# Reloads moved from GpSimd to ScalarE, U's copy taken from PSUM, and first loads on two queues, in a two-block transformer kernel

## The chip, the cores and the metric

The kernel runs on one core of one Trainium2 chip. The metric is the device time of one execution in microseconds (us). Three runs of the kernel before gave 2861.27, 2851.15 and 2854.03 us, median 2854.03. The profiled execution, from which all times in the prediction come, took 2851.9 us.

The names used below: PE is TensorE (matmuls and transposes), ACT is ScalarE, DVE is VectorE, POOL is GpSimd, SP is SyncE, which here only issues transfers. Each engine works through its own instructions in a fixed order. A DMA is issued by an instruction of one of these engines and then runs by itself.

## The reference, cut to what matters

The input is one sequence of 256 tokens of width 2048, all in float32. Two transformer blocks follow each other. The first mixes RWKV-7 time mixing (16 heads) with dilated attention (16 heads):

```python
def first_block(x, ...):
    u = rms_norm(x, norm1_g)
    q, k, v, z = split(u @ w_in)                       # attention 3 x 1024, RWKV 3360 columns
    attn = dilated_attention(q, k, v, rel_bias_table)  # three windows, joined by their log-sum-exp
    rw = rwkv7_time_mix(z, ...)
    h = x + concat([attn, rw]) @ w_out
    return rms_norm(h + ffn(rms_norm(h)), final_g)

def rwkv7_step(state, inp):                            # 256 steps, one after the other
    r, w, k, v, a, bb = inp
    sa = einsum('bhij,bhj->bhi', state, a)
    state = state * w + sa[..., None] * bb + v[..., None] * k
    y = einsum('bhij,bhj->bhi', state, r)
```

`rwkv7_time_mix` ends with a group norm of y over each head (mean, variance, reciprocal root), a bonus term and a gate. The second block has three other attention branches, a gated merge and a feed-forward part with a short convolution. Its order of work is not touched here.

## The kernel before, in words

**The weight products.** Nearly all of the time goes into `lin` (L299): out[256, n] = x @ W in float32 precision, made of three products in a faster number format. Of each weight tile of 128x512 float32 (`raw`, loaded by SP, 512 KB for two tiles, three buffers), ACT casts the high part `wh` (L332, three buffers), DVE subtracts the low part `wl` (L333, two buffers), and PE multiplies x's high part by `wh` and by `wl`, and x's low part by `wh`: six matmuls of 512 columns for a weight tile, three for each half of the tokens (L219). The x tiles themselves are split once into high and low parts; for the first block this is `load_T` (L1104), which loads x transposed in eight pieces, splits each on ACT (L1114) and DVE (L1115), then loads x in its natural order and squares it on ACT (L254) for the row norm.

**RWKV in chunks.** The 16 heads are done in four groups of four heads. For each group, keys, receptances and values are brought in from a DRAM spool (`spool`, L982; w_in's products are written there by ACT, and `load`, L997, brings them back as kA, rA, vA for group 1, kB, rB, vB for groups 2 and 3), transposed on PE into `zt`, and turned into matrices over chunks of 32 tokens: D, BKT and others (`rwkv_pairs`). For each chunk a triangular system has to be solved: `solve_T` (L578) sends D through DRAM (scN) into a layout N, runs 62 small dependent operations on POOL (31 multiplications X, L594, and 31 additions T, L596), and sends the result through DRAM (scT) to the tile TTx, of which there is one. Then `chain` (L604) runs the eight chunks, each depending on the one before. One step of it is: a D matmul (`ch<-UV,D`), copies Xc by DVE and ACT (L625, L626), a TTx matmul (`ch<-Xc,TTx`), copies into UV by DVE and ACT (L628, L629), a BKT matmul (`ch<-UV,BKT`), a copy of U into Ux by POOL (L636), a matmul `ch<-Ux,D`, the new state S on DVE (L640, L641) and the output copy Y on ACT (L644), with which the next step's `ch<-S,ARx` begins. All the matmuls of a step write into one PSUM tile, `ch`. There are 32 steps in all, 8 for each of 4 groups.

**After a chain.** `rwkv_out` (L650) does the group norm of Y on DVE and ACT, transposes it on PE (`yt`), multiplies by the gate (`g` on PE) and gives `rw`. For groups 0 to 2 POOL writes rw to DRAM (`mixd`, L687) and later loads it back as `mx` (L1078), as it does with the attention outputs; ACT and DVE split it into `mixh` and `mixl` (L1084, L1085), the inputs of the output product `lin("w_out")`. Group 3's rw is split in place. Pairs of k-tiles of w_out stand for the pieces: 10 and 11 for the last attention quarter, 12 and 13 for group 2, 14 and 15 for group 3.

**What sets the order.** The program is written stage by stage. A scheduler with a model of time then puts all instructions of a core in an order for each engine, with `high_priority(SPLIT_AHEAD)` drawing the raw loads and weight splits of `lin` forward. So independent `lin` matmuls stand on PE between the steps of a chain. Once built, each engine keeps its order: an instruction that waits holds up all those behind it on its engine, DMA issues too. The reloads of kA and the others, the mx loads, the solver and the Ux copies all stand in POOL's one order.

**Startup.** `pv` (a table of gains and other small parameters) is loaded by POOL; ACT issues the eight loads of x transposed (`x<-in_xT` in the profile) and the eight of x natural; POOL clears many tiles (memsets, L383 and others).

Of the kernel before, what the change touches and what calls it, by code (L numbers as in the profile page):

```python
# [19 lines left out]
P = 128  # L20
S = 256
# [66 lines left out]
NPV = _c  # L88
# [96 lines left out]
class Builder:  # L185
    def __init__(self, ctx, tc, A, dbg=None):
# [9 lines left out]
        self.woff = {}  # L196
        self.pvt = self.load_const("pv", [P, NPV], eng=self.nc.gpsimd)
        self.ident = self.load_const("c_ident", [P, P], eng=self.nc.gpsimd)
# [151 lines left out]
class Block1(Builder):  # L350
# [253 lines left out]
    def chain(self, st):  # L604
# [10 lines left out]
        for c in range(8):  # L615
# [15 lines left out]
            if c < 7:  # L631
# [3 lines left out]
                l = lc[:, :, c, :].to_broadcast([P, 2, 64])  # L635
            nc.gpsimd.tensor_copy(Ux[0:64], by(st.UV)[0:64, :, c, :])  # L636
            for p in range(2):
# [329 lines left out]
class Kernel(Block2):  # L967
# [14 lines left out]
    def spool(self, name):  # L982
# [14 lines left out]
        def load(half):  # L997
            t = self.slot([P, 2, S], name)
            nc.gpsimd.dma_start(t, d[:, :, half * S:(half + 1) * S])
            return t  # L1000
# [5 lines left out]
    def block1_mix(self):  # L1006
        nc, tc = self.nc, self.tc
        with tc.tile_pool(name="ring1", bufs=1) as self.ring, tc.tile_pool(name="p1", bufs=1) as self.p1:
            self.NW, self.NWL = 3, 2
            xT = self.new_xT("x")  # L1010
            ss = self.new_ss("x", 8)
            self.load_T(xT, "x", "norm1_g", ss, nc.scalar)
            rs = self.row_rstd(ss, "x")
# [3 lines left out]
            self.lin("w_in", 0, xT, self.nat_evac(lo, rs))  # L1017
            self.rwkv_consts()
            self.lora_lo(lo)
# [83 lines left out]

    def load_T(self, xT, name, gain, ss, queue):  # L1104

        nc = self.nc
        hi, lo = xT
        for c in range(8):
            t = self.slot([P, 2, S], name) if name == "x" else self.stage(name)
            queue.dma_start(t, self.A[name + "T"][:, 2 * c:2 * c + 2, :])  # L1110
            for j in range(2):
                kt = 2 * c + j
                g = self.pv(gain, kt)
                nc.scalar.activation(hi[:, kt, :], t[:, j, :], AF.Identity, scale=g)  # L1114
                nc.vector.scalar_tensor_tensor(lo[:, kt, :], t[:, j, :], g, hi[:, kt, :].bitcast(F32),  # L1115
                                               op0=ALU.mult, op1=ALU.subtract)
        for c in range(8):
            t = self.stage(name)
            queue.dma_start(t, self.A[name][:, c * S:(c + 1) * S].rearrange("(t p) c -> p t c", p=P))
            for tb in range(2):  # L1120
                self.square(ss, t[:, tb, :], tb, c)
# [4 lines left out]
    def mem_kv(self):  # L1126
# [3 lines left out]
        ss = self.new_ss("mem", 8)  # L1130
        self.load_T(xT, "mem", "g_mem_2", ss, nc.gpsimd)
        rs = self.row_rstd(ss, "mem")
# [193 lines left out]
```

## Time and profile before

| | |
|---|---|
| runs | 2861.27, 2851.15, 2854.03 us, median 2854.03 |
| profiled execution | 2851.9 us, of which the span of the profile is 2850.1 |
| PE busy | 2773.8 us, 97% of the span |
| DVE, ACT, POOL busy | 1741.2 (61%), 1550.3 (54%), 179.7 (6%) |
| DMA | 534.37 MB, mean 187 GB/s |

In the profile's lists a row names the line, the engine and the operation, `out<-in` by the program's tile names; `x12` counts instructions. In a timeline a row begins with the start and the duration in us, and `[4.53 <-DMA kA<-sp_kA]` says that the engine stood idle for 4.53 us before it, until this transfer had landed. PE shows as busy from a matmul's start to its modelled end, and matmuls overlap. PEld is the loading of the stationary operand, PEclk the granted TensorE clock as a share of full speed.

### The profile page before, as it was taken

Reading aid. Unit: us, or ns where it says so; the run is one execution under the profiler, and the core shown is the slowest. Engines: PE = TensorE matmul, PEld = TensorE weight load, DVE = VectorE, ACT = ScalarE, POOL = GpSimd, SP = SyncE. Lnnn points to the kernel's source line nnn. Section 1 sums busy time; section 2 is a strip of 40 time slices with the busy share of each in tenths; the row PEclk is TensorE's granted clock in tenths of the full one; section 3 lists DMA queues with packets and bytes.
Section 4 is the critical chain, followed back from the end, with each engine's and each line's share of the span. In section 5 each row is a group of like instructions: output and inputs, shape, how many; then the busy total and the mean of one; then the engine's idle time right before and its main releaser. Section 6 shows DMA issues by size and latency. Waiting matters only on the chain.

```text
span 2850.1 us, 40071 instructions
## 1 busy us (share of the span) xinstructions
PE 2773.8 (97%) x13496; PEld 2320.1 (81%) x13496; DVE 1741.2 (61%) x3088; ACT 1550.3 (54%) x2847; POOL 179.7 (6%) x395
## 2 busy tenths in 40 slices
PE   7989989999999999999999999999999999999999
PEld 6877877777888888888888888888888888888887
DVE  5665756557555555555666666666666666667554
ACT  5544546546544445454555664455556666666444
POOL 2034043300000000000000000000000000000000
PEclk9999999999999999999999999999999999999999
DMA  6755556565666666666655556666555555555665
GB/s 212 208 166 169 179 153 204 168 217 175 191 191 190 188 189 190 192 190 191 217 174 181 163 170 193 199 203 196 190 184 188 185 185 185 185 184 185 200 201 168
DMA packets 168663, 534.37 MB, mean 187 GB/s; under 512 B 31041, under 2 KB 36167, under 8 KB 168456
## 3 DMA queue, kind: packets, MB, share of 16 engines
q1 hardware_dynamic: 149404, 487.90, 54.7%
q0 software_dynamic: 7360, 25.28, 2.9%
q10 hardware_dynamic: 11692, 18.63, 2.0%
q8 instruction: 106, 1.74, 0.3%
q14 instruction: 101, 0.83, 0.1%
HBM read 518.07 MB, written 16.82 MB: 188 GB/s over the span
## 4 chain that ended last, share of the span: by engine, by line
PE 89%; DMA 4%; POOL 2%; issue 2%; DVE 2%; ACT 1%; SPq 0%; ACTq 0%; DVEq 0%; POOLq 0%
PE lin L219 83%; PE ch L648 1%; POOL T L596 1%; POOL X L594 1%; PE tr L224 1%; PE uT L224 1%; DMA scN<-D 1%; DMA N<-scN 1%; DVE wl L333 0%; DMA x<-in_xT_dram 0%; PE o L219 0%; PE D L219 0%; DMA raw<-in_w_out_dram 0%; DMA mem<-in_memT_dram 0%; PE lg L219 0%
## 5 line engine op out<-in xcount | busy, mean ns | idle before, releaser
L333 DVE TENSOR_TENSOR wl<-raw,wh 128x512 fp32r<-128x512 f32 (+2 forms) x1848 | 1268.1, 689 | 891.9 <-PE lin L219 780.9
L332 ACT CAST wh<-raw 128x512 fp32r<-128x512 f32 (+2 forms) x1848 | 1138.9, 618 | 1098.5 <-PE lin L219 1027.8
L219 PE MATMUL lin<-wl,x2h 128*128 128x512 f32 (+2 forms) x800 | 293.3, 369 | 3.1 <-DVE wl L333 3.1
L219 PE MATMUL lin<-wh,x2l 128*128 128x512 f32 (+2 forms) x800 | 289.4, 364 | 0.0
L219 PE MATMUL lin<-wl,u2h 128*128 128x512 f32 x704 | 281.0, 399 | 0.0
L219 PE MATMUL lin<-wl,hhi 128*128 128x512 f32 x704 | 275.0, 391 | 0.0
L219 PE MATMUL lin<-wh,u2l 128*128 128x512 f32 x704 | 274.3, 390 | 0.0
L219 PE MATMUL lin<-wh,hlo 128*128 128x512 f32 x704 | 273.9, 389 | 0.0
L219 PE MATMUL lin<-wl,uh 128*128 128x512 f32 x704 | 273.9, 391 | 0.0
L219 PE MATMUL lin<-wh,ul 128*128 128x512 f32 x704 | 272.7, 390 | 0.4 <-DVE ul L291 0.4
L219 PE MATMUL lin<-wh,x2h 128*128 128x512 f32 (+2 forms) x800 | 244.9, 365 | 1.6 <-ACT wh L332 1.2
L219 PE MATMUL lin<-wh,uh 128*128 128x512 f32 x704 | 227.7, 391 | 1.0 <-ACT uh L290 0.9
L219 PE MATMUL lin<-wh,u2h 128*128 128x512 f32 x704 | 225.6, 392 | 0.0
L219 PE MATMUL lin<-wh,hhi 128*128 128x512 f32 x704 | 219.9, 389 | 0.0
L219 PE MATMUL lin<-wl,xh 128*128 128x512 f32 (+2 forms) x512 | 191.5, 378 | 8.1 <-DVE wl L333 8.0
L219 PE MATMUL lin<-wh,xl 128*128 128x512 f32 (+2 forms) x512 | 180.2, 356 | 0.0
L219 PEld LDWEIGHTS lin<-wl,x2h 128*128 128x128 f32 x800 | 150.8, 189 | 29.1 <-DVE wl L333 6.1
L219 PE MATMUL lin<-wh,xh 128*128 128x512 f32 (+2 forms) x512 | 154.0, 359 | 18.3 <-ACT wh L332 18.3
L219 PEld LDWEIGHTS lin<-wh,x2h 128*128 128x128 f32 x800 | 148.0, 188 | 26.5 <-ACT wh L332 1.8
L219 PEld LDWEIGHTS lin<-wh,x2l 128*128 128x128 f32 x800 | 150.9, 189 | 22.8
L219 PEld LDWEIGHTS lin<-wh,uh 128*128 128x128 f32 x704 | 132.1, 188 | 29.6 <-ACT uh L290 1.7
L219 PEld LDWEIGHTS lin<-wh,u2h 128*128 128x128 f32 x704 | 132.2, 188 | 27.9
(428 smaller groups left out, 3786.8 us busy)
## 6 DMA issues: line engine op xcount, KB each, us to landing
raw<-in_w_in_dram SPq DMA_DIRECT2D x268, 512.0 KB, 3.8
raw<-in_w_gate_up_dram SPq DMA_DIRECT2D x176, 512.0 KB, 3.8
raw<-in_w_down_dram SPq DMA_DIRECT2D x176, 512.0 KB, 4.0
raw<-in_w_up_dram SPq DMA_DIRECT2D x176, 512.0 KB, 3.6
raw<-in_w_out_dram SPq DMA_DIRECT2D x64, 512.0 KB, 3.7
raw<-in_w_mem_kv_dram SPq DMA_DIRECT2D x16, 512.0 KB, 4.2
raw<-in_w_br_fox_dram SPq DMA_DIRECT2D x12, 512.0 KB, 4.2
raw<-in_w_br_sb_dram SPq DMA_DIRECT2D x12, 512.0 KB, 4.3
```

The source lines that it names most:

```text
L219: self.nc.tensor.matmul(out, lhsT=lhsT, rhs=rhs, start=start, stop=stop)
L224: self.nc.tensor.transpose(out, in_, self.ident[p0:p0 + n, p0:p0 + n])
L332: nc.scalar.copy(wh[:, :m * n], raw[:, cs])
L333: nc.vector.tensor_tensor(wl[:, :m * n], raw[:, cs], wh[:, :m * n].bitcast(F32), op=ALU.subtract)
L594: gp.tensor_tensor(x, T[:, 0:m, u:u + 1].to_broadcast([P, m, n]), N[:, u:u + 1, u + 1:32].to_broadcast([P, m, n]), op=ALU.mult)
L596: gp.tensor_tensor(w, w, x, op=ALU.add)
L648: self.nc.tensor.matmul(out, lhsT=lhsT, rhs=rhs, start=start, stop=True, skip_group_check=True)
```

## The change

Three parts are changed.

1. **First loads.** pv is loaded by ACT, as its first transfer. All eight loads of x transposed are issued ahead of the splits, alternately by ACT and by SP (between SP's first raw weights). The RWKV constants (with POOL's memsets) stand between the splits of x and the natural loads, and the natural loads are issued by POOL. `SPLIT_AHEAD = 100` draws the first weight splits forward.
2. **U's copy.** Ux is written by one ACT copy and one DVE copy of 64x64, each straight from the PSUM tile `ch`, where POOL copied 64x128 out of UV. In the built program the ACT copy waits for the BKT matmuls on PE, which write the same PSUM tile, the DVE copy waits for the ACT copy, and the matmul `ch<-Ux,D` for the DVE copy.
3. **Reloads.** kA, rA, vA, kB, rB, vB (kB, rB and vB twice) are issued by ACT.

```diff
-        self.pvt = self.load_const("pv", [P, NPV], eng=self.nc.gpsimd)
+        self.pvt = self.load_const("pv", [P, NPV], eng=self.nc.scalar)
...
-            nc.gpsimd.tensor_copy(Ux[0:64], by(st.UV)[0:64, :, c, :])
+            nc.scalar.copy(Ux[0:64, 0, :], ch[0:64, 128:192])
+            v.tensor_copy(Ux[0:64, 1, :], ch[64:128, 128:192])
...
         def load(half):
             t = self.slot([P, 2, S], name)
-            nc.gpsimd.dma_start(t, d[:, :, half * S:(half + 1) * S])
+            nc.scalar.dma_start(t, d[:, :, half * S:(half + 1) * S])
...
-            self.load_T(xT, "x", "norm1_g", ss, nc.scalar)
+            self.SPLIT_AHEAD = 100
+            self.load_T(xT, "x", "norm1_g", ss, (nc.scalar, nc.sync), self.rwkv_consts)
...
-            self.rwkv_consts()
             self.lora_lo(lo)
...
-    def load_T(self, xT, name, gain, ss, queue):
+    def load_T(self, xT, name, gain, ss, queues, between=None):
...
+        def load(c):
+            ts.append(self.slot([P, 2, S], name) if between else self.stage(name))
+            queues[c % len(queues)].dma_start(ts[c], self.A[name + "T"][:, 2 * c:2 * c + 2, :])
+
+        if between:
+            for c in range(8):
+                load(c)
         for c in range(8):
-            t = self.slot([P, 2, S], name) if name == "x" else self.stage(name)
-            queue.dma_start(t, self.A[name + "T"][:, 2 * c:2 * c + 2, :])
+            if not between:
+                load(c)
+            t = ts[c]
...
+        if between:
+            between()
         for c in range(8):
             t = self.stage(name)
-            queue.dma_start(t, self.A[name][:, c * S:(c + 1) * S].rearrange("(t p) c -> p t c", p=P))
+            nc.gpsimd.dma_start(t, self.A[name][:, c * S:(c + 1) * S].rearrange("(t p) c -> p t c", p=P))
```

The change also moves instructions in the scheduler's order. Three places matter to the prediction.

**PE at the end of group 2's chain.** Numbers behind a name tell one tile from the next: before, `ch_4250` is group 3's chain, `Y_3908` group 2's output, and group 2's chain has ended ahead of the first row. The rows before:

```order
L219 MATMUL lin_5731<-wh_5832,mixl_5650 128x512
L224 MATMUL ot_5156<-k_c_ident,on_5075 128x128 x2
L648 MATMUL ch_4250<-UV_4060,BKT_4059 128x64 x2
L648 MATMUL ch_4250<-Ux_402,D_4058 128x64 x2
L224 MATMUL yt_4230<-k_c_ident,Y_3908 128x128 x4
L219 MATMUL g_4231<-gT,gup 128x256 x4
L648 MATMUL ch_4250<-S_4261,ARx_397 128x64 x2
L648 MATMUL ch_4250<-UV_4060,D_4058 128x64 x2
```

The rows of the changed kernel, where `ch_3925` is group 2's chain and `ch_4274` group 3's:

```order
L649 MATMUL ch_3925<-Xc_4027,TTx 128x64
L219 MATMUL lin_5924<-wh_5928,mixh_5681 128x512
L649 MATMUL ch_3925<-UV_3409,BKT_3408 128x64 x2
L649 MATMUL ch_3925<-Ux_159,D_3407 128x64 x2
L649 MATMUL ch_3925<-S_4035,ARx_152 128x64 x2
L649 MATMUL ch_3925<-UV_3409,D_3407 128x64 x2
L649 MATMUL ch_3925<-Xc_4047,TTx 128x64
L649 MATMUL ch_3925<-UV_3409,BKT_3408 128x64 x2
L649 MATMUL ch_3925<-Ux_158,D_3407 128x64 x2
L649 MATMUL ch_3925<-S_4055,ARx_152 128x64 x2
L649 MATMUL ch_3925<-UV_3409,D_3407 128x64 x2
L649 MATMUL ch_3925<-Xc_4067,TTx 128x64
```

Behind these come `ch_3925<-Ux_159` (group 2's last), four entries of group 3's chain, group 2's `yt` and `g`, seven more entries of group 3's chain, and only then the next weight matmul, of k-tile 12. Between group 2's last `ch<-Ux` and its `yt` there stood 28 weight matmuls of 512 columns before; there stands none now. In an average step of the chains 2.5 weight matmuls stood between the BKT matmul and `ch<-Ux`; there stand 10.1 now.

**PE at the end of group 3's chain**, the last one. The rows before, in which the last `ch<-Ux` is 58 weight matmuls ahead of `yt`:

```order
L219 MATMUL lin_6216<-wh_6362,mixh_5649 128x512
L219 MATMUL lin_6217<-wh_6362,mixl_5650 128x512
L224 MATMUL yt_5706<-k_c_ident,Y_4249 128x128 x4
L219 MATMUL g_5707<-gT,gup 128x256 x4
L219 MATMUL lin_6407<-wh_6411,mixh_5649 128x512
```

The rows of the changed kernel:

```order
L219 MATMUL lin_6248<-wh_6394,mixl_5682 128x512
L219 MATMUL lin_6249<-wl_6395,mixh_5681 128x512
L219 MATMUL lin_6249<-wh_6394,mixl_5682 128x512
L649 MATMUL ch_4274<-Ux_159,D_4082 128x64 x2
L224 MATMUL yt_5738<-k_c_ident,Y_4273 128x128 x4
L219 MATMUL g_5739<-gT,gup 128x256 x4
L219 MATMUL lin_6439<-wh_6443,mixh_5681 128x512
```

The last `ch<-Ux` stands directly ahead of `yt` now.

**POOL around the last solver**, where mx loads for w_out's k-tiles 6 to 11 are issued. Before, they follow the solver's last addition:

```order
L594 TENSOR_TENSOR X_4131<-T_4130,N_4125 128x8
L596 TENSOR_TENSOR T_4130<-T_4130,X_4131 128x8
L636 COPY Ux_402<-UV_3393 64x128
L745 DMA toep_5116<-toepd 128x2x384
L1078 DMA mx_5663<-mixd 128x512
L1078 DMA mx_5667<-mixd 128x512
```

In the changed kernel they stand inside the solver, the first of them after 40 of its 62 operations:

```order
L596 TENSOR_TENSOR T_4154<-T_4154,X_4155 128x5x12
L1079 DMA mx_5695<-mixd 128x512
L594 TENSOR_TENSOR X_4155<-T_4154,N_4149 128x66
L1079 DMA mx_5699<-mixd 128x512
L596 TENSOR_TENSOR T_4154<-T_4154,X_4155 128x6x11
L594 TENSOR_TENSOR X_4155<-T_4154,N_4149 128x60
```

From group 3's last D matmul, with which this solver's input begins, to the first weight matmul whose cast stands behind the cast of `mx_5663` on ACT (k-tile 4) PE had 148 weight matmuls and 99 smaller ones before; it has 74 and 59 now, counted to the cast behind `mx_5695`. Elsewhere, from group 0's last D matmul to the first use of TTx PE had 152 and 43, and has 146 and 43; from group 2's last D matmul to the first use of the attention keys nk it had 139 and 48, and has 133 and 57.

More of the change, by code (lines that the diff above doesn't have):

```diff
@@ L1102, in block1_out @@
             self.rs_h = self.row_rstd(ss, "h")
-    def load_T(self, xT, name, gain, ss, queue):
+    def load_T(self, xT, name, gain, ss, queues, between=None):
         nc = self.nc
         hi, lo = xT
+        ts = []
+        def load(c):
[4 more added lines that the diff above has]
+                load(c)
         for c in range(8):
-            t = self.slot([P, 2, S], name) if name == "x" else self.stage(name)
-            queue.dma_start(t, self.A[name + "T"][:, 2 * c:2 * c + 2, :])
+            if not between:
+                load(c)
+            t = ts[c]
             for j in range(2):
@@ L1130, in mem_kv @@
         ss = self.new_ss("mem", 8)
-        self.load_T(xT, "mem", "g_mem_2", ss, nc.gpsimd)
+        self.load_T(xT, "mem", "g_mem_2", ss, (nc.gpsimd,))
         rs = self.row_rstd(ss, "mem")
```

## The prediction

> **What bounds the kernel now.** I read the page first, then stretches of the span, then who waited for whom on PE, then timelines at the places found. The page:
>
> ```profile
> PE 2773.8 (97%) x13496; PEld 2320.1 (81%) x13496; DVE 1741.2 (61%) x3088; ACT 1550.3 (54%) x2847; POOL 179.7 (6%) x395
> ```
>
> PE sets the time; what can be won is what it idles. The stretches (start:end, length, then busy time and count of PE, PEld, DVE, ACT, POOL, then the granted clock, the DMA share and GB/s):
>
> ```profile
> 0.00:40.00 40.00, 20.70 (x124) 18.86 (x125) 22.52 (x58) 23.90 (x71) 14.36 (x29) 0.99 0.77 259
> 140.00:160.00 20.00, 14.00 (x52) 10.45 (x51) 9.41 (x16) 7.24 (x14) 16.81 (x44) 0.83 0.40 121
> 220.00:240.00 20.00, 15.97 (x69) 12.85 (x69) 8.71 (x16) 6.45 (x14) 16.95 (x44) 0.83 0.42 127
> 380.00:400.00 20.00, 16.20 (x76) 13.14 (x75) 10.98 (x21) 9.02 (x19) 17.30 (x41) 0.91 0.36 104
> 400.00:440.00 40.00, 34.38 (x160) 28.27 (x159) 27.14 (x64) 16.87 (x36) 14.43 (x34) 0.87 0.50 157
> 540.00:560.00 20.00, 16.34 (x88) 13.88 (x87) 11.25 (x34) 7.86 (x19) 2.74 (x6) 0.87 0.44 141
> 700.00:2850.00 2150.00, 2141.08 (x9995) 1781.62 (x9993) 1305.19 (x2166) 1177.27 (x2024) 7.10 (x8) 1.00 0.60 188
> ```
>
> From 700 us on PE runs 9995 matmuls in 2150 us, 0.215 us each, at full clock: nothing to win, and the change doesn't touch it. All that can move lies in the first block. There the poor stretches have two losses: idle time, and a clock of 0.83 to 0.91 afterwards. In 220 to 240 PE idles 4.0 us, and at 0.215 us its 69 matmuls would have taken 15, so I count up to 5 lost there. Three of these stretches have POOL busy for 17 of 20 us, by its solver. PE's waits, in us, times, longest:
>
> ```profile
> PE lin L219 <- ACT wh L332: 25.3, 7, 15.3
> PE ch L648 <- POOL Ux L636: 8.1, 3, 3.3
> PE zt L224 <- DMA kA<-sp_kA: 4.5, 1, 4.5
> PE qkt L224 <- DMA nk<-sp_k: 3.6, 3, 2.8
> PE ch L648 <- DMA TTx<-scT: 3.2, 2, 2.7
> ```
>
> The first is mostly the start (15.3). The others are what the change aims at: Ux copies and reloads that stand behind the solver on POOL.
>
> **First loads.**
>
> ```profile
> 8.49 4.87 DVE L361 TENSOR_SCALAR k_omix<-k_pv 128x27 f32<-128x27 f32 x1 [8.49 <-DMA k_pv<-in_pv_dram]
> 12.26 0.97 POOL L565 MEMSET UV<- 64x1024 f32 x1
> ```
>
> The small DVE operation begins when pv lands at 8.49 and ends at 13.36, when POOL's clearing ends (12.26 + 0.97 = 13.2). DVE, not the loads alone, holds the first xl. The natural x loads and their 16 squares move behind more work, and the row norm made of them gates the evacuation of the first product, so a gain ahead of it is mostly waited off there. The DMA share is 0.77 already. The gain is bounded by the excess of 15.3 us over pv's landing, less the casts, so about -3; the loss by natural loads on POOL that come late, +4. I take +1, since the squares' gate is nearer. The Trainium skill, page DMA: Bandwidth & Descriptors, section "Issuing engines are not separate DMA queues", says that transfers from several issuers run on the same 16 DMA engines and that spreading them saves only the issue time. By it this term would be about 0, by the rows above up to -3; the DMA share of 0.77 agrees with it.
>
> **Reloads of group 1.** These are rows of POOL, and one of PE:
>
> ```profile
> 139.25 0.38 POOL L594 TENSOR_TENSOR X<-T,N 128x31 f32<-128x31 f32 x1 [7.24 <-DMA N<-scN]
> 145.15 0.76 POOL L999 DMA_DIRECT2D kA<-sp_kA  x1
> 166.59 0.75 POOL L999 DMA_DIRECT2D rA<-sp_rA  x1 [0.43 <-DMA raw<-in_w_in_dram]
> 168.26 0.72 POOL L726 DMA_DIRECT2D nq<-sp_q  x1
> 170.72 0.63 POOL L596 TENSOR_TENSOR T<-T,X 128x8 f32<-128x8 f32 x1
> 179.44 0.43 PE L648 MATMUL ch<-Xc,TTx 128*128 128x64 f32 x2 [0.57 <-DMA TTx<-scT]
> ```
>
> kA's wait of 4.5 goes, or shrinks. But what is late next is TTx: PE already waits 0.57 for it at 179.44. The solver's start is set by D (through DRAM), which stands at the same place of PE's order as before. So PE, freed of 4.5 us, stands at TTx instead. Only the solver's own shortening counts: four issues leave it (kA, rA, vA, nq: 4 x 0.73 plus the 0.43 ahead of rA = 3.4), while PE's work from D to TTx has fallen by 6 matmuls (1.3 us), so that of the 3.4 only 2.1 is gained. A longer wait in one piece leaves a slower clock behind it, about 2 by the stretches above. I take 0; bounds -3 and +2. Moved loads can also hold ACT: kB, rB and vB are issued a few rows behind the stores that they read, with casts behind them. A store takes 3 to 5 us to land and three `wh` buffers cover about 4 us of PE. Three places, 0 to 1.3 each: +1.5.
>
> **Ux off POOL.** The waits of 8.1 in three places, with their clock: 220 to 240 loses 5, up to 8 with what spills beyond it: -7 (-5 to -8), since nothing else stands behind it. The one in 380 to 400 is followed by nk and TTx:
>
> ```profile
> 388.56 0.75 POOL L999 DMA_DIRECT2D kB<-sp_kB  x1
> 413.00 0.75 POOL L999 DMA_DIRECT2D rB<-sp_rB  x1
> 414.46 0.72 POOL L726 DMA_DIRECT2D nk<-sp_k  x1
> ```
>
> nk is still a POOL load behind the solver. It comes earlier by kB, rB, vB and two Ux copies (3 x 0.74 + 0.6 = 2.8); PE would be earlier by more, so again it waits, for nk. TTx's 2.7 goes, since the chain's first use now stands far later. I take -6 for 380 to 440 (idle 3.8 + 5.6, of which nk's longer wait stays; -3 to -8). The third Ux wait, near 492: -3 with its clock (-1.5 to -3.5).
>
> **The new step.** One bare step of the chain before, without cover:
>
> ```profile
> 550.08 0.61 PE L648 MATMUL ch<-UV,D 128*128 128x64 f32 x4
> 552.11 0.43 PE L648 MATMUL ch<-Xc,TTx 128*128 128x64 f32 x2 [1.42 <-ACT Xc L626]
> 552.84 0.21 ACT L629 COPY UV<-ch 64x64 f32<-64x64 f32 x1 [0.77 <-DVE UV L628]
> 553.10 0.66 PE L648 MATMUL ch<-UV,BKT 128*128 128x64 f32 x4 [0.55 <-ACT UV L629]
> 553.59 0.61 PE L648 MATMUL ch<-Ux,D 128*128 128x64 f32 x4
> ```
>
> From TTx's matmul to BKT's it takes 0.99: matmul, DVE copy, ACT copy after it. From BKT's to `ch<-Ux` 0.49 before, as POOL worked meanwhile; now two copies one after the other stand between, the same 0.99 plus a longer matmul: 1.2. [...] In this trace the ACT copy into UV does start only after the DVE copy. Under weight matmuls (10.1 per step) this hop costs PE nothing. A bare step costs 1.0 + 1.0 + 1.2 + 1.3 (S, two DVE operations of 0.3, then the matmul) = 4.5.
>
> **Emptied stretch at group 2's end.** The cover was taken from later places. Before, its tail ran so:
>
> ```profile
> 537.42 0.26 ACT L644 COPY Y<-ch 64x128 f32<-64x128 f32 x1
> 546.73 0.69 DVE L664 TENSOR_TENSOR Y<-Y,gn 128x512 f32<-128x512 f32 x1
> 547.47 0.66 PE L224 MATMUL yt<-k_c_ident,Y 128*128 128x128 f32 x4 [0.51 <-DVE Y L664]
> 552.55 0.55 POOL L687 DMA_DIRECT2D mixd<-rw  x1 [0.28 <-issue]
> 555.85 0.54 POOL L1078 DMA_DIRECT2D mx<-mixd  x1 [2.39 <-DMA mixd<-rw]
> 558.93 0.61 ACT L1084 CAST mixh<-mx 128x512 fp32r<-128x512 f32 x1
> ```
>
> Y to `yt` is 10.05 with other DVE work between; bare I take 7. `yt` to mixh's end is 12.1, a serial way through DRAM. With the last matmul, 20 in all. PE's cover before was 28 + 12 weight matmuls (8.6) and 43 short ones (6.5 at the 0.15 of ch's four in 0.61): 15, which leaves 5, and 540 to 560 shows 3.7 idle. Now the tail has only the short ones, 5, so 15 stay bare, and the chain's last three steps ahead of it, ten hops at about 1.0, are bare too: 10 less 3 of own matmuls. That is 15 + 7 - 5 = +17 (+8 if the group norm and the hops run at half of this; +22 with longer queues).
>
> **Loads inside the last solver.**
>
> ```profile
> 472.32 1.05 PE L219 MATMUL D<-ARx,BKx 128*128 128x128 f32 x8
> 486.40 0.23 POOL L594 TENSOR_TENSOR X<-T,N 128x31 f32<-128x31 f32 x1 [5.42 <-DMA N<-scN]
> 517.20 0.21 POOL L596 TENSOR_TENSOR T<-T,X 128x8 f32<-128x8 f32 x1
> ```
>
> D to the solver's start is 13, the solver 31. The first mx load behind 40 of 62 operations comes 13 + 20 = 33 after D, lands 3 later, and its cast holds the weight casts behind it on ACT until 36.6. PE's work to there has gone from 148 + 99 matmuls to 74 + 59, about 26. So PE idles up to 10; it is late itself by some waits: +5 (0 to +10).
>
> **Emptied stretch at group 3's end.**
>
> ```profile
> 620.33 0.26 ACT L644 COPY Y<-ch 64x128 f32<-64x128 f32 x1 [0.18 <-PE ch L648]
> 636.54 0.60 PE L224 MATMUL yt<-k_c_ident,Y 128*128 128x128 f32 x4
> ```
>
> 58 weight matmuls (12.5) covered the last group norm; none does now. The last matmul, Y and 7 of group norm are bare, plus about 1 for the clock: +8 (+5 to +11).
>
> **The sum**: +1 + 0 + 1.5 - 7 - 6 - 3 + 17 + 5 + 8 = +16.5, against the profiled 2851.9 (span 2850.1 and 1.8 around it): 2868. The median of the runs shown, 2854.03, is 2.1 above the profiled one.
>
> **Rivals.**
> 1. Faster: the removed waits count whole and the emptied stretches are half hidden. kA's and vA's waits with their clock go (-7.5), if the solver gets N earlier, then -7 - 6 - 3; the loads cost nothing (0), the start 0, reloads +1.5, the stretches +8 and +5. That is -9, 2843. For it: POOL is freed of 32 copies and 12 issues. Against: TTx's wait of 0.57 at 179.44, which shows the solver right behind. It decides from the point where the stretches cost less than 16 together.
> 2. No change: 0 for group 1, -16 of Ux as forecast, +1 and +1.5, the stretches +8 and +5, loads 0: -0.5, 2851. For it: the cover in the order is a plan; PE that comes later to the stretch finds the group norm's engines freer. Against: the tail is serial, and it starts with PE's own last matmul.
> 3. Slower still: ACT held by three stores in full (+4), the mx loads whole (+10), the first stretch +22, the last +11, the start +4: with -16, +35, 2887. For it: ACT's queue carries copies of each step. Against: needs all at once.
> 4. The change doesn't do what it says: pv and x land no sooner (the rule on queues above). Then the start's term is 0 and the time 2867; it is a part of the forecast.
>
> **How the numbers follow.** Forecast with its neighbours 0.52 and rival 3 0.08: slower by over 0.3% (8.6 us, about what a measurement of this kernel can tell from no change) 0.60. Rival 2 with all that falls within 2845.5 to 2862.6: 0.23. Rival 1: 0.17. The forecast's own range, from bounds that won't all fall one way, is 2855 to 2880. The range for 8 in 10 takes in rival 2 and half of the way to rival 1, and leaves out most of rival 3: 2847 to 2882.
>
> **What would show it.** Right: PE waiting for TTx at group 1's chain by 4 us or more, no wait for POOL Ux anywhere, PE waiting 15 us or more in all between group 2's last steps and k-tile 12 (rows `ch <- DVE Ux`, `yt <- DVE Y`, `lin <- ACT mixh`), and some 7 us ahead of the last `yt`. Wrong: a first TTx without a wait, or those two stretches with less than 16 us of idle time together, or ACT standing long in its reload issues; then the sum's largest terms are mis-sized.

## The result, and the profile after

Four runs of the changed kernel took 2884.08 to 2889.86 us, median 2886.60. The kernel before took 2851.15 to 2861.27 us beside them, median 2854.91. The ratio is 1.0109, 95% interval 1.0087 to 1.0132: the change makes the kernel slower by 25 to 38 us. The forecast was 2868 us, with a range of 2847 to 2882, so the direction was right and the size was outside the range.

The profiled execution took 2884.52 us, its span 2882.8 us, against 2850.1 before. These are its busy times, which answer to the first row shown of before:

```profile
PE 2790.2 (97%) x13496; PEld 2330.9 (81%) x13496; DVE 1750.7 (61%) x3120; ACT 1557.4 (54%) x2879; POOL 173.6 (6%) x361
```

PE runs the same 13496 matmuls and is busy for 16 us longer, though no matmul was added. So half of the loss does not show as idle time. The mean granted clock is 0.984, against 0.992 before. The stretches of the span show where matmuls run slowly (start:end, length, then PE, PEld, DVE, ACT, POOL busy and count, the granted clock, DMA share, GB/s). After:

```profile
160.00:180.00 20.00, 11.55 (x54) 9.04 (x53) 10.68 (x17) 7.46 (x14) 13.43 (x31) 0.89 0.47 134
220.00:240.00 20.00, 17.80 (x89) 14.56 (x88) 12.76 (x23) 10.08 (x21) 17.40 (x36) 1.00 0.54 159
250.00:270.00 20.00, 17.06 (x81) 14.47 (x80) 8.69 (x20) 6.41 (x16) 1.12 (x2) 0.83 0.52 167
560.00:620.00 60.00, 51.72 (x224) 43.21 (x224) 27.04 (x67) 21.61 (x52) 3.10 (x5) 0.76 0.42 130
700.00:2850.00 2150.00, 2145.23 (x10016) 1785.36 (x10015) 1309.30 (x2180) 1185.88 (x2039) 7.08 (x8) 1.00 0.60 189
```

And the same stretches of before, as far as they were not shown:

```profile
160.00:180.00 20.00, 17.66 (x89) 14.01 (x88) 16.51 (x36) 12.55 (x22) 10.07 (x22) 1.00 0.76 223
250.00:270.00 20.00, 20.00 (x114) 17.30 (x113) 12.10 (x27) 10.40 (x27) 1.84 (x3) 1.00 0.54 165
560.00:620.00 60.00, 60.00 (x312) 50.98 (x311) 30.30 (x58) 28.33 (x58) 3.63 (x9) 0.99 0.56 175
```

The stretch at 220 to 240 is mended as forecast: 89 matmuls at full clock where there were 69 at 0.83. But 160 to 180 and 250 to 270, which were nearly full and full before, now lose 35 and 33 matmuls. And 560 to 620 loses 88, with a granted clock of 0.76. From 700 us on nothing has changed.

To compare places in two kernels whose orders differ, I use one number, PE's **arrears**. Each matmul is given the distance at which its kind (the tile that it writes, and its shape) is followed undisturbed in the trace of before (0.227 us for 512 columns, 0.111 for a step of the chain, and so on). The arrears at a point are the time of the span so far, less the sum over all matmuls issued so far. The point is given by that sum, so that it is the same amount of PE work in every kernel. The second row names what stands there in the kernel before. The arrears come from one profiled execution of each kernel, and executions of one kernel differ by several us (19 of the kernel before took 2847.64 to 2863.63). So a few us between two kernels are a hint and no proof.

| PE work done (us) | 25 | 80 | 165 | 250 | 422 | 480 | 542 | end |
|---|---|---|---|---|---|---|---|---|
| what stands there | first product | D of group 0 | group 0's chain | group 1's chain | group 2's chain | k-tile 12 | last `yt` | |
| before | 24.9 | 31.1 | 46.0 | 54.6 | 80.6 | 90.9 | 94.8 | 123.4 |
| after | 28.9 | 32.4 | 50.8 | 61.7 | 80.5 | 117.6 | 125.6 | 155.8 |
| difference | +4.0 | +1.3 | +4.8 | +7.1 | -0.1 | +26.7 | +30.8 | +32.4 |

The late loss was forecast well: from 422 to the end +32.5, where the sum had +30. The early gain is what is missing: at 422 there should have been a lead of some 14 us, and there is none.

**The early part.** PE's waits, in us, times, longest:

```profile
PE qkt L224 <- DMA nq<-sp_q: 7.8, 2, 7.7
PE lo L224 <- ACT lo L409: 7.0, 1, 7.0
PE yt L224 <- DVE Y L665: 6.9, 1, 6.9
PE qkt L224 <- DMA nk<-sp_k: 6.8, 1, 6.8
PE ch L649 <- DVE Ux L637: 3.3, 5, 1.0
PE ch L649 <- DMA TTx<-scT: 0.7, 1, 0.7
```

The waits for Ux from POOL and for kA are gone. In their place stand `lo` at the start, nq and nk. Timelines at these places, of POOL, PE, SP and ACT (start, duration, and in brackets the idle time before and what ended it):

```profile
142.47 0.64 POOL L594 TENSOR_TENSOR X<-T,N 128x31 f32<-128x31 f32 x1 [6.73 <-DMA N<-scN]
174.26 0.21 POOL L596 TENSOR_TENSOR T<-T,X 128x8 f32<-128x8 f32 x1
174.77 0.76 POOL L727 DMA_DIRECT2D nq<-sp_q  x1 [0.29 <-issue]
178.17 1.11 PE L224 MATMUL qkt<-k_c_ident,nq 128*128 128x128 f32 x4 [7.67 <-DMA nq<-sp_q]
183.34 0.41 PE L649 MATMUL ch<-Xc,TTx 128*128 128x64 f32 x2 [0.72 <-DMA TTx<-scT]
...
247.36 2.56 SPq L598 DMA_DIRECT2D scT<-T  x4
250.02 1.49 SPq L323 DMA_DIRECT2D raw<-in_w_in_dram  x3
254.01 1.14 ACT L332 CAST wh<-raw 128x512 fp32r<-128x512 f32 x2 [5.78 <-DMA raw<-in_w_in_dram]
254.68 1.22 PE L219 MATMUL lin<-wh,xh 128*128 128x512 f32 x2 [2.94 <-ACT wh L332]
```

The first solver (group 0's, beside which group 1's kA, rA and vA are reloaded) runs from 142.47 to 174.47, 32.0 us. Before, it ran from 139.25 to 171.35, 32.1 us. Four issues left it and it did not get shorter. nq is now issued behind the solver's last operation, and PE idles for it. In the second solver the same happens on another queue: SP's transfer scT waits for the solver to end, and the weight loads behind it on SP wait too. ACT then stands 5.78 us without a weight tile, and PE 2.94. This solver takes 31.9 us (215.42 to 247.33) where it took 29.5 (211.45 to 240.99), so that it ends 6.3 us later than before. By the arrears, before loses 7.9 us between 218 and 237, mostly to the wait for Ux and the slow clock behind it. The changed kernel loses 3.0 us between 218 and 234, where PE waits 1.47 and 0.74 us for low parts from DVE, and 6.4 us between 250 and 272. What PE gains ahead of these two solvers, it gives back.

**The late part.** First the mx loads inside the last solver, then two steps of group 2's chain, which now stand without other work on PE, and what follows:

```profile
528.77 0.59 POOL L1079 DMA_DIRECT2D mx<-mixd  x1 [0.18 <-issue]
531.77 0.62 ACT L1085 CAST mixh<-mx 128x512 fp32r<-128x512 f32 x1 [7.79 <-DMA mx<-mixd]
532.96 1.22 PE L219 MATMUL lin<-wh,mixh 128*128 128x512 f32 x2 [4.38 <-ACT wh L332]
...
551.66 0.56 PE L649 MATMUL ch<-UV,BKT 128*128 128x64 f32 x4
552.25 0.21 ACT L636 COPY Ux<-ch 64x64 f32<-64x64 f32 x1 [0.75 <-PE ch L649]
552.49 0.23 DVE L637 COPY Ux<-ch 64x64 f32<-64x64 f32 x1 [1.24 <-ACT Ux L636]
552.77 0.66 PE L649 MATMUL ch<-Ux,D 128*128 128x64 f32 x4 [0.56 <-DVE Ux L637]
557.80 1.12 PE L649 MATMUL ch<-UV,BKT 128*128 128x64 f32 x4 [0.55 <-ACT UV L629]
573.91 1.11 PE L224 MATMUL yt<-k_c_ident,Y 128*128 128x128 f32 x4
579.70 0.59 POOL L688 DMA_DIRECT2D mixd<-rw  x1 [38.55 <-issue]
585.49 0.62 ACT L1085 CAST mixh<-mx 128x512 fp32r<-128x512 f32 x1 [1.72 <-DMA mx<-mixd]
667.27 1.09 PE L224 MATMUL yt<-k_c_ident,Y 128*128 128x128 f32 x4 [6.92 <-DVE Y L665]
```

ACT stands 7.79 us for an mx tile that POOL issued from inside the solver, the weight cast behind it comes late, and PE waits 4.38 us. From 535 to 542 the granted clock is 0.58. By the arrears this place costs 8.9 us more than before.

The hop BKT, ACT copy, DVE copy, Ux takes 1.1 us at full clock, as forecast. The tail through DRAM and the wait ahead of the last `yt` are there too. The sum had a term for the clock only at group 3's end ("about 1 for the clock"). Here the clock shows in BKT's four matmuls, which take 0.56 at 551.66 and 1.12 at 557.80: the gaps of the bare steps, 0.4 to 1.4 us each, are enough to halve PE's clock (0.50 from 555 to 560), so that PE's own part of a bare step takes twice as long.

### The profile page after: what moved, and what is told of

It reads as the page before. It is cut to its first block, busy times and chain, and to the rows that moved or that the text cites. A ratio compares the mean times of both kernels' runs of the same rounds, so it can differ in the third digit from the quotient of the medians.

```text
span 2882.8 us, 40078 instructions
## 1 busy us (share of the span) xinstructions
PE 2790.2 (97%) x13496; PEld 2330.9 (81%) x13496; DVE 1750.7 (61%) x3120; ACT 1557.4 (54%) x2879; POOL 173.6 (6%) x361
## 4 chain that ended last, share of the span: by engine, by line
PE 77%; DVE 1%; DMA 0%; issue 0%; ACT 0%; DVEq 0%; ACTq 0%
PE lin L219 74%; PE tr L224 1%; PE uT L224 1%; PE o L219 0%; PE ch L649 0%; DVE wl L333 0%; PE pT L224 0%; DMA cb<-cd 0%; PE sl L219 0%; DVE R L941 0%; DMA cd<-cT 0%; PE ml L219 0%; DMA mx<-mixd 0%; PE g L219 0%; PE fl L219 0%
```

## The experiments

All ratios are to the kernel before, with the 95% interval.

**The parts one by one.** First each of the three parts alone, and the two without U's copy.

```diff
 # e1: before, with
-            nc.gpsimd.tensor_copy(Ux[0:64], by(st.UV)[0:64, :, c, :])
+            nc.scalar.copy(Ux[0:64, 0, :], ch[0:64, 128:192])
+            v.tensor_copy(Ux[0:64, 1, :], ch[64:128, 128:192])
 # e2: before, with
-            nc.gpsimd.dma_start(t, d[:, :, half * S:(half + 1) * S])
+            nc.scalar.dma_start(t, d[:, :, half * S:(half + 1) * S])
 # e3: before, with the new load_T, its call and pv on ScalarE
 # e4: the changed kernel, with U's copy as before
```

> The kernel before with the second part of the change alone (Ux written by ACT and DVE from the PSUM tile). Theory A: the loss sits in this part, by the order it brings: group 2's chain ends bare ahead of its yt, group 3's too, and mx loads stand inside the last solver. Then it is slower by 22 to 32 us, with over 15 us of PE idle between group 2's last steps and k-tile 12, about 7 us ahead of the last yt, and no wait for POOL Ux. Rival B: the loss comes from the reloads and natural loads that changed queues, ACT held and POOL late. Then this one is within 8 us of before.

> The kernel before with the third part alone (reloads issued by ACT). Theory A: near nothing, -3 to +5 us: kA's wait of 4.5 us goes and the wait turns up at nq and TTx behind group 0's solver; the Ux waits of POOL stay. Rival B: slower by 10 us or more, with PE waiting for ACT casts behind reload issues.

> The kernel before with the first part alone (first loads on two queues, natural loads on POOL, first splits ahead). Theory A: +1 to +5 us, all within the first 40 us: the first matmul some 7 us earlier than 15.3, then one wait of about 7 us for lo, since the natural loads and so the squares come late; behind it the order is as before. Rival B: more than +5, or losses beyond 60 us. Rival C, that this part does what it says: -3 us or better.

> The changed kernel without its second part (Ux copied by POOL as before, the first and third part kept). Theory A: the sum of the two parts alone, 0 to +9 us, and the stretch from group 2's last steps to k-tile 12 idle by under 8 us as before. Rival B: over +15 us.

| run | median us | ratio |
|---|---|---|
| e1 Ux alone | 2880.73 | 1.0081 (1.0063 to 1.0099) |
| e2 reloads alone | 2857.03 | 0.9998 (0.9987 to 1.0009) |
| e3 first loads alone | 2855.47 | 0.9997 (0.9984 to 1.0011) |
| e4 reloads and first loads | 2857.99 | 0.9997 (0.9986 to 1.0008) |

U's copy carries the loss; the other two parts make no difference that can be measured. In e1 the arrears are 72.2 at 422, so 8.4 are won early, and 121.1 at 542, so 34.7 are lost late. Both halves of the mechanism are there. PE idles some 13 us between group 2's last steps and k-tile 12 in it, where over 15 was expected; the rest is clock. e3's time lies between what its theories A and C had. e1 also shows who keeps the early gain down: kB, still issued by POOL in it, costs PE 5.83 us at 383, where Ux had cost 3.29.

**The first loads.** In e3 the first matmul starts at 8.29 us in place of 15.28, and nothing comes of it, because of the wait for `lo`. In the changed kernel ACT squares natural x until 37.64, before until 31.98, since the natural loads come later. e7 is e3 with the natural loads issued by ACT:

```diff
-            nc.gpsimd.dma_start(t, self.A[name][:, c * S:(c + 1) * S].rearrange("(t p) c -> p t c", p=P))
+            (nc.scalar if name == "x" else nc.gpsimd).dma_start(t, self.A[name][:, c * S:(c + 1) * S].rearrange("(t p) c -> p t c", p=P))
```

> The part with the first loads alone (2855.5, no difference), but the eight loads of natural x are issued by ScalarE, as before, and not by GpSimd. Theory A (the 7 us that were won ahead of the first matmul were lost again in the wait of 7.0 us for lo, because natural x comes late from GpSimd's queue): the wait for lo is under 4 us, and the run is 2848 to 2853. Theory B (the loads as a whole set when lo can be evacuated, on any queue): the wait stays at 6 to 8 us, and the run is 2853 to 2858.

It took 2855.98 us, 1.0004 (0.9994 to 1.0013), and PE's wait for `lo` was 5.2 us. The time is theory B's; the wait lies between the numbers of the two. POOL's queue is worth 1.8 of the 7.0 us, the rest stays with ACT as the issuer too, and the time doesn't move.

**The engines or the place of the copy.** This is the question that the prediction had not asked. In the change two things are new at once: ACT and DVE copy instead of POOL, and the copy waits for the BKT matmuls, which write the same PSUM tile. e5 keeps the engines and takes the source from SBUF; e9 keeps engines and PSUM source and puts the two lines ahead of the BKT matmuls.

```diff
 # e5: before, with
-            nc.gpsimd.tensor_copy(Ux[0:64], by(st.UV)[0:64, :, c, :])
+            nc.scalar.copy(Ux[0:64, 0, :], UV[0][0:64])
+            v.tensor_copy(Ux[0:64, 1, :], UV[1][0:64])
 # e9: e1, with the lines moved up
             Ux = self.Ux[c % 2]
+            nc.scalar.copy(Ux[0:64, 0, :], ch[0:64, 128:192])
+            v.tensor_copy(Ux[0:64, 1, :], ch[64:128, 128:192])
             if c < 7:
                 for p in range(2):
                     self.acc(ch[:, 256 + 64 * p:320 + 64 * p], st.BKT[:, 8 * p + c, :], UV[p])
...
-            nc.scalar.copy(Ux[0:64, 0, :], ch[0:64, 128:192])
-            v.tensor_copy(Ux[0:64, 1, :], ch[64:128, 128:192])
```

> The kernel before with one edit: U's copy is made by ScalarE and VectorE, but from UV in SBUF, which is there before the state matmul of the step, not from the PSUM bank that the state matmul also writes. The numbers of instructions on ScalarE and VectorE are those of the run with the Ux part alone (2881 us), but the plan stays near that of before: the chains of groups 2 and 3 end at their old places with other work between their steps. Theory A (the loss of the Ux part is the emptied stretch that the plan makes behind the new place of the copy): 2843 to 2858, no wait for Ux above 4 us on GpSimd's account at 220 to 240 and 380 to 440, and no stretch at half clock near 560 to 620. Theory B (the loss is the copies' own time on ScalarE and VectorE, in front of the holds and mixh): 2870 to 2885, with the waits for mixh and Y of the Ux run.

> The Ux part alone (2881 us), with the two copies of U from PSUM written ahead of the state matmuls of the step and not behind them. Source, engines and number of the copies are as in the change; only the place differs, so that the copies don't wait for the state matmul that writes the same bank. The plan then ends chain 2 near its old place. Theory A (the loss is the step of the chain made longer by the hop behind the state matmul, which the plan answers with bare steps at the end): 2840 to 2858, as the run with the copies from SBUF, and no stretch at half clock at 550 to 620. Theory B (reading PSUM while TensorE writes the bank, or the copies ahead of UV, cost it): 2868 to 2885.

| run | median us | ratio | weight matmuls between BKT and Ux, mean of 28 steps | arrears at 250, 422, 480, 542 |
|---|---|---|---|---|
| before | 2855.4 to 2856.7 | | 2.5 | 54.6, 80.6, 90.9, 94.8 |
| e1 | 2880.73 | 1.0081 | 10.4 | 56.8, 72.2, 113.2, 121.1 |
| e5 | 2844.71 | 0.9958 (0.9940 to 0.9976) | 0.4 | 52.9, 71.7, 85.2, 85.9 |
| e9 | 2847.59 | 0.9970 (0.9957 to 0.9982) | 0.0 | 51.8, 72.2, 90.2, 90.8 |

Theory A holds in both, and both runs beat the kernel before and the changed one. The stretch at 560 to 620, of e5 and then of e9:

```profile
560.00:620.00 60.00, 60.00 (x311) 50.86 (x311) 32.78 (x68) 29.80 (x65) 3.78 (x6) 1.00 0.73 233
```

```profile
560.00:620.00 60.00, 60.00 (x302) 50.70 (x301) 30.98 (x65) 29.39 (x64) 3.41 (x6) 0.96 0.66 202
```

It is full, with 311 and 302 matmuls. Neither the engines nor the reading of PSUM cost anything that these runs can tell: e9 has exactly the two copies of e1, five lines higher, and is 33 us faster. The scheduler answers the hop behind BKT by putting 10 weight matmuls into it in each step. That uses up the cover, and the chains end later in PE's order: group 2's last TTx matmul comes after 448 us of PE's work before, and after 464 us in the changed kernel. Its output, the way through DRAM and group 3's chain then stand bare. With the copy ahead of BKT the order is nearly that of before (448 in e5, 453 in e9). No run has the late copies in the old order, so what the hop alone would cost there is open. One step of e5 in its timeline shows the two copies side by side, ahead of BKT:

```profile
553.69 0.24 ACT L636 COPY Ux<-UV 64x64 f32<-64x64 f32 x1
553.82 0.19 DVE L637 COPY Ux<-UV 64x64 f32<-64x64 f32 x1 [1.40 <-ACT UV L629]
554.07 0.55 PE L649 MATMUL ch<-UV,BKT 128*128 128x64 f32 x4
554.46 0.61 PE L649 MATMUL ch<-Ux,D 128*128 128x64 f32 x4
554.99 1.02 PE L219 MATMUL lin<-wh,mixh 128*128 128x512 f32 x2
```

The Trainium skill, page PSUM — Partial Sum Buffer, section "PSUM bank collisions raise a hardware error", asks that two engines which touch one bank in the same 32 partitions, at whatever address, be kept apart by semaphores. Its section "Summary: rules for kernel authors" advises to read another bank than the one that a running matmul writes. The traces show what the first costs: from the shared tile the ACT copy starts behind BKT (551.66, 552.25), from SBUF both copies start ahead of it (553.69 and 553.82, BKT at 554.07). That the DVE copy from the shared tile also waits for the ACT copy (552.49) is the built program's order. The two read different halves of the partitions, so the rule does not ask for it. No run here used another bank.

**No copy at all.** Ux's lower 64 rows are never filled by the copy, so the matmul can read the upper 64 rows of UV itself.

```diff
 # e6: before, with
-            nc.gpsimd.tensor_copy(Ux[0:64], by(st.UV)[0:64, :, c, :])
...
-                self.acc(xy[p], D[:, 8 * p + c, :], Ux[:, p, :])
+                self.acc(xy[p], D[0:64, 8 * p + c, :], UV[p][0:64])
 # e8: e7 with the same edit
```

> The kernel before with no copy of U at all: the step's output matmul reads the 64 upper rows of UV and of D directly, since the lower 64 rows of Ux multiply into nothing. It takes the 28 copies off GpSimd and puts them nowhere. Theory A (the waits for Ux near 220 to 240 and 380 to 440 are worth their length, and nothing else in the Ux part is good or bad but the plan): 2838 to 2850, a gain of 4 to 16. Theory B (what is won before a solver is lost behind it again, as in the run of the whole change, where nothing was left at the end of group 3): 2848 to 2857, no difference, with new waits of 3 to 7 us for the loads that are issued behind the solver (nk, nq) or for weights.

> The two edits together: no copy of U (matmul over 64 rows), and the first loads on two queues with natural x on ScalarE. If both gain by their own and the gains add: 2832 to 2847. If group 1's solver is the bound of the early part, so that a sooner start only makes PE wait longer for nq and TTx behind it: the same as the run without U's copy alone, within 3 us.

e6 took 2854.15 us, 0.9993 (0.9983 to 1.0002), and e8 2853.72 us, 0.9995 (0.9985 to 1.0004): theory B's time for e6, no difference, and nothing from the start on top of it. The 32 copies are gone from POOL, and the new waits behind the solvers are those for kB (4.5 us) and rA (2.6), more than for nq and nk. Yet e5, which has two copies more in each step, is 9 us faster than e6. Up to 8 us of this can lie in the matmuls over 64 rows (see the last section); how much the order adds was not tried.

**Pairs of parts.** e10 is the whole change with e5's source, e11 the change without the new first loads, e12 the change without the moved reloads.

```diff
 # e10: the changed kernel, with
-            nc.scalar.copy(Ux[0:64, 0, :], ch[0:64, 128:192])
-            v.tensor_copy(Ux[0:64, 1, :], ch[64:128, 128:192])
+            nc.scalar.copy(Ux[0:64, 0, :], UV[0][0:64])
+            v.tensor_copy(Ux[0:64, 1, :], UV[1][0:64])
 # e11: e1 with e2's line
 # e12: the changed kernel, with
-            nc.scalar.dma_start(t, d[:, :, half * S:(half + 1) * S])
+            nc.gpsimd.dma_start(t, d[:, :, half * S:(half + 1) * S])
```

> The whole change, with U's copies from UV in SBUF in place of PSUM. Theory A (the first loads and the reloads on ScalarE are worth nothing on their own and take away some of the gain of a faster copy): 2843 to 2855, above the 2845 of the SBUF copies alone. Theory B (they add, since the copies no longer stand late): 2834 to 2842.

> The changed kernel without its first part: reloads on ScalarE and U's copies from PSUM as in the change, first loads as before. The whole change loses 32 us, the Ux part alone 26. If the remaining 6 us are an interaction of the reloads with U's copies (nq and nk behind the solver, raw behind scT): 2884 to 2891, with waits for nq or nk of 6 us and more, and the early part without the gain of the Ux part alone. If they are the start's: 2876 to 2882.

> The changed kernel without its second part: first loads and U's copies as in the change, reloads on GpSimd as before. If the interaction is with the reloads: 2877 to 2883, as the Ux part alone. If the start is what costs the remaining 6 us: 2884 to 2891.

| run | median us | ratio | arrears at 165, 250, 422, 542 |
|---|---|---|---|
| e1 Ux | 2880.73 | 1.0081 (1.0063 to 1.0099) | 49.3, 56.8, 72.2, 121.1 |
| e11 reloads and Ux | 2886.03 | 1.0113 (1.0098 to 1.0128) | 51.0, 61.6, 82.6, 127.2 |
| e12 first loads and Ux | 2884.57 | 1.0109 (1.0092 to 1.0126) | 52.3, 60.8, 76.1, 126.3 |
| the whole change | 2886.60 | 1.0109 (1.0087 to 1.0132) | 50.8, 61.7, 80.5, 125.6 |
| e10 the whole with SBUF copies | 2849.81 | 0.9986 (0.9977 to 0.9995) | 53.2, 62.2, 82.3, 98.2 |

The 4 to 6 us beyond e1 come with either part, and not twice with both: e11 and e12 each came out as the reading has it that blames their own part. The intervals touch that of e1, so that the times can't lay it on one part. The arrears hint at where it goes: with the reloads on ACT the early gain of 8.4 us is gone at 422 (82.6 in e11), by waits of 7.85 us for nq and 6.5 for nk. With the first loads in place of the reloads 4 us of it are gone (76.1 in e12). e10 is in its theory A's range, 5 us slower than e5, and has lost its gain by 422 too (82.3 against 71.7); but its profiled execution, of 2856.44 us, is the slowest of its ten.

**The queue or the solver.** Is nq late because it stands behind the solver on POOL, or would PE wait as long for the solver itself? In e13 the changed kernel issues the attention's loads from ACT; e14 is the same edit in e5.

```diff
-            nc.gpsimd.dma_start(t, sp[2][:, :, cs])
+            nc.scalar.dma_start(t, sp[2][:, :, cs])
```

> The changed kernel with the attention's loads (nq, nk, nv) issued by ScalarE and not by GpSimd, so that they don't stand behind a solver. Theory A (GpSimd's queue is the cause of the lost early gain): the waits for nq and nk near 170 and 411 fall from 7.7 and 6.9 us to under 3, no wait for TTx of over 2 us takes their place, and the run is 2872 to 2881. Theory B (the solver's result is the bound, and the load only stands in front of it): waits for TTx, for raw's weights or for kB of the same sum come in their place, and the run is 2882 to 2890.

> The faster version (U's copies from SBUF, 2845) with the attention's loads issued by ScalarE. Its waits for nq are 4.2 us in all and for TTx 3.1. Theory A: 2839 to 2844. Theory B (the solver is the bound, or ScalarE's queue is late): 2843 to 2850.

e13 took 2899.56 us, 1.0152 (1.0136 to 1.0167), above the range of both theories; e14 took 2848.53 us, 0.9968 (0.9954 to 0.9982), as its theory B has it, where e5 had 2844.71. In e13's timeline the two waits are gone, and PE stands as long a little behind:

```profile
169.15 0.60 PE L224 MATMUL qkt<-k_c_ident,nq 128*128 128x128 f32 x4
183.37 0.66 PE L649 MATMUL ch<-Xc,TTx 128*128 128x64 f32 x2 [10.40 <-DMA TTx<-scT]
...
419.50 0.21 POOL L596 TENSOR_TENSOR T<-T,X 128x8 f32<-128x8 f32 x1
419.73 2.54 SPq L598 DMA_DIRECT2D scT<-T  x4
422.38 6.56 SPq L323 DMA_DIRECT2D raw<-in_w_in_dram  x4
426.98 1.22 PE L219 MATMUL lin<-wh,xh 128*128 128x512 f32 x2 [6.53 <-ACT wh L332]
```

PE transposes nq at 169.15, nine us sooner, and starts the chain at 183.37, where the whole change had 183.34. At this place the solver is the bound, as theory B has it; the load only stood in front of it. At the second place PE no longer waits 6.85 us for nk, but 6.53 for weights that stand behind scT on SP. Why e13 is 13 us slower than the whole change is only seen in part: its arrears at 422 are 93.5, with a further new wait of 4.9 us for UV near 254, and I did not separate ACT's issues from the changed order.

## Why the prediction was wrong

Taken by the steps of its sum, each against the difference of the arrears over the same piece of PE work:

| step of the sum | forecast | measured | piece |
|---|---|---|---|
| first loads | +1 | +1.3 | to 80 |
| group 1's reloads | 0 | +3.5 | 80 to 165 |
| Ux at 220 to 240 | -7 | +2.3 | 165 to 250 |
| Ux at 380 to 440 and near 492 | -9 | -7.2 | 250 to 422 |
| ACT's holds at kB, rB and vB | +1.5 | within the two rows above | 210 to 285 |
| group 2's emptied end, and the mx loads | +22 | +26.8 | 422 to 480 |
| group 3's emptied end | +8 | +4.1, and +1.6 behind it | 480 to the end |
| sum | +16.5 | +32.4 | |

**The step that failed is the -7 for Ux at 220 to 240.** "Since nothing else stands behind it" was wrong. The wait itself did vanish, but PE then waited for DVE's low parts and for weight tiles whose loads stand behind scT on SP, which waits for the end of this solver. At the first solver the prediction had seen that PE, freed of one wait, stands at the next, and for nk too; at this place it had only looked at PE's own list, and not at what SP's queue holds behind the solver. This accounts for 9.3 of the 15.9 us. Even in e5 and e9 the gain in this piece is only some 4 us, with waits of 1.17 and 1.78 us for the same weights. No run took scT or the weight loads off SP, so this step is read from the traces alone.

**Group 1's reloads** were right in kind, though the prediction called the chain at this place group 1's, and it is group 0's. PE stands behind the solver, and e13 shows it by moving the wait from nq to TTx with the start of the chain unchanged within 0.03 us. Two things were off. The wait was forecast at TTx, and is at nq for the most part, since nq also moved behind the solver's end. And the solver was to become 3.4 us shorter by four issues that leave it, but it stayed at 32 us, so nothing of the 2.1 us of gain came.

**ACT's holds** cost PE nearly nothing: ACT idles up to 2.2 us around the issues of kB, rB and vB, and PE waits 0.47 us in all there. The stores ahead of these loads land in 2.4 to 3.4 us in the profile of before, where the prediction had 3 to 5.

**The emptied end of group 2** was right in its place and mechanism, with the hop at 1.1 us against 1.2 forecast. Its size, 22 with the mx loads, was 4.8 too low. The mx loads cost 8.9 where +5 stood, the 4.38 us of waiting and the slow clock behind it. The emptied end cost 19.9 where +17 stood. Its tail was well sized: from group 2's last `ch<-Ux` (565.67) to the first matmul of k-tile 12 (586.16) it takes 20.5 us, 20 forecast. The steps ahead of it were not: they lose 10.8 us where 7 stood. There the clock was left out: the sum added the hops to PE's own time at full speed, and in the trace that own time doubles (0.56 to 1.12). Ahead of both, 1.9 us are won, since before waits for nq and nk near 508. The Trainium skill, page TensorE: Matmul & The Clock Gate, section "Part 1: The HAM clock gate", says that the clock halves after idle windows of about 3.4 us and by how busy the array has been. Here no gap of the stretch was longer than 1.41 us; the trace agrees with the second half of the rule and shows that a string of short gaps is enough.

**Group 3's end** was 2.3 too high: 6.92 us of idle time ahead of `yt`, of which 7 were forecast, but the arrears of before rise by 3.9 in this piece too.

**The rivals.** Rival 3 had 2887, almost the time measured, but not its way, so its number is luck: it kept the -16 of Ux, of which 4.9 came, and needed ACT held by its reloads, +4, while in the trace the reloads themselves hold PE for 0.6 us at most (vA). Rival 1 (waits gone count whole) falls by the first of its conditions, a solver that starts or ends sooner. Rival 4, that the first loads come no sooner, falls too: the first matmul starts 7.2 us sooner, and it was the row norm that gave it back, as the forecast said.

**The signs.** Of the signs for being right, the wait for POOL's Ux is gone and 6.9 us stand ahead of the last `yt`. But TTx is waited for 0.72 us, not 4, and PE idles some 12 us between group 2's last steps and k-tile 12, not 15; the rest of the loss there is PE's own time at half clock.

**What the forecast took for fixed.** The order was read as it was in the built program, and the loss was derived from it step by step. It did not ask which line of the change makes the order so. e9 answers this: not the engines, and not PSUM, but the place of the two copies behind the matmuls that write the same tile.

## What to carry to other kernels

Before a copy is moved from an SBUF source to PSUM, look at which tile it reads and who writes that tile next in the program: a copy that stands behind a matmul into the same tile waits for it, and a scheduler may pay for that wait with cover that is needed elsewhere. The same two copies five lines higher turned a loss of 24 us into a gain of 8.

When a stall ahead of a serial piece of work (here the solver) is removed, ask what every queue holds behind that piece, SP's weight loads included, before the stall is counted as won: here nq, nk, raw and TTx took its place one after the other.

## What the runs showed of the hardware that I had not expected

**POOL's small operations have two speeds.** In the solver of the changed kernel the same operation on the same shape takes 0.27 us in one place and 0.61 in another:

```profile
407.12 1.37 DVE L550 TENSOR_TENSOR BKx<-sq,linv 64x512 f32<-64x512 f32 x2
408.02 0.61 POOL L594 TENSOR_TENSOR X<-T,N 128x42 f32<-128x42 f32 x1
536.35 0.27 POOL L594 TENSOR_TENSOR X<-T,N 128x42 f32<-128x42 f32 x1
```

At 408.02 DVE works beside it on two tiles in SBUF, at 536.35 DVE is idle. Of the 248 operations of the changed kernel's four solvers, 168 have DVE busy for more than 0.3 of their time and take 0.49 us in the mean, the others 0.27 (80); before the change it is 0.47 and 0.29. What DVE does matters too: 115 operations beside DVE's work on two SBUF tiles take 0.57, and 53 beside its other work 0.33. The Trainium skill, page SBUF — State Buffer, section "SBUF: two separate sides", says that DVE and GpSimd share a pair of ports and that the one which comes second is blocked for a whole instruction, where DVE has two inputs in SBUF and GpSimd reads SBUF; these means agree with it. It would explain why the solver gets no shorter when issues leave it: PE idles less beside it, so DVE subtracts more weight tiles (its busy share beside the first solver rises from 0.58 to 0.75). No run took DVE's work away, so this is argued and not shown.

**A change of the matmul's height costs time on PE.** In e6, where a matmul over 64 rows follows one of BKT over 128 rows, its start comes 0.205 us after it (27 places), the second of 64 rows 0.160 after the first, and the next matmul of 128 rows 0.202 after the last of 64 (32 places each, medians). Neighbours of one height are 0.112 apart, and a weight matmul follows one of the chain in 0.084 in e5. So I estimate 0.26 us for each step, some 8 us for the 32 steps, where no wait hides it. The rows of one step, with four matmuls in each of the first two:

```profile
571.65 0.55 PE L647 MATMUL ch<-UV,BKT 128*128 128x64 f32 x4
572.13 0.66 PE L647 MATMUL ch<-UV,D 64*128 64x64 f32 x4
572.72 0.50 PE L219 MATMUL lin<-wl,mixh 128*128 128x512 f32 x1
```

The four matmuls of BKT take 0.48 to the next here and 0.39 in e5's rows above. The Trainium skill, page TensorEngine Tiling (Array Packing), section "Key Properties", says that a change of tiling mode drains the engine; it gives no figure, and these rows agree with it.
